# Key products shared between GpSimd and VectorE in a hybrid decoder step

## Chip, cores and metric

The kernel runs on one core of a Trainium2 chip. The metric is the device time of one execution in microseconds. Five engines matter: TensorE (PE; its weight loads are PEld), VectorE (DVE, `V` in the code), ScalarE (ACT, `S`), GpSimd (POOL, `G`) and SyncE (SP, `Q`), which issues most of the DMAs.

## What is computed

One inference step of a decoder trunk of two layers (`DEPTH` 2, `D_MODEL` 1024) for a prompt of 512 rows and for 8 samples of 8 rows, which share the weights. Cut to what matters, with the cache used by the sample rows alone:

```
h = rmsnorm(x, norm1); proj = h @ w_in
q, k, v, u, ga, gb = split(proj)             # 12 heads of 64, 3 groups of 4
o_a = dilated_mixture(rope(q), [cache; rope(k)], [cache; v])   # windows 128/1, 512/4, 2048/16
o_b = pool_branch(u)                         # causal means over 2, 4, 8, 16 rows
x = x + (sigmoid(ga) * (o_a @ w_pa) + sigmoid(gb) * (o_b @ w_pb)) @ w_o
x = x + square(relu(rmsnorm(x, norm2) @ w_up)) @ w_down
```

The scores of a sample row are dot products of its query with cached keys. Per pair of heads (`p` = 0 or 1) the kernel forms them without TensorE, as a product of keys and a broadcast query, summed over the 64 elements of each head.

## The kernel before

All activations are held transposed, as 8 tiles of 128 x 576 (512 prompt columns and 64 sample columns). Weights arrive as `raw` tiles; ScalarE rounds a tile to `wh`, VectorE subtracts to get the rest `wl`, and TensorE multiplies three times per weight (`wnext`, `wplain`, `gemm`, `gemm8`). So every weight tile needs one ScalarE pass and one VectorE subtraction with two SBUF inputs.

Per layer the order on TensorE is: the qkv units d, a, b, e, c of p = 0 and then d, a, b, c of p = 1 (`qkv`), four gates u for the pooling branch, eight gates gb with their projections of `ob`, eight gates ga with their projections of `oat` (these begin with `until("D", 1)`, that is, after the decode attention of p = 1), the output projection, and the MLP.

Beside this main order run side generators, resumed at each `tick` of the main order: `unit_out` (evacuates a qkv unit: `nat` on ScalarE, `dn` on VectorE), `prompt(p)` (attention of the prompt: scores `sp`, row maxima, `exps`, a small chain `xt`, `ex`, `ct`, `cc`, then `weigh`, `flip`, `pv`), `decode(p, qb)` (attention of the samples), `windows` and `lin` (pooling branch). The program order on every engine is the order of emission. A planner decides it: each engine is a `Lane` with a modelled time `t`, advanced by a fixed cost and a rate; a generator yields the modelled time at which it wants to go on (`after`, `ready`, or a number of us). `Lane` models what GpSimd does to VectorE in one line: a VectorE instruction with more than one large SBUF input is lengthened, to at most 1.4 times its streaming time, while GpSimd is modelled busy.

`decode` for one `p` does this. It loads keys in chunks `kc` (one of 8 rows per lane of window 128, and alternately windows 512 and 2048 for c = 0..3). For each c and each of the three groups it forms two products `prod` (tokens c and c + 4) on GpSimd, 128 x 1024 for two groups and 128 x 512 for the third, so 24 per `p` and 96 in all; `fold` sums each on VectorE with a `tensor_reduce` into `SC`, one to two products behind; the generator goes on every 2.2 us (1.1 us for the small ones). `prod` has three buffers. Then follow the products with the new keys (`prodn`, VectorE), the softmax of `SC`, and the weighted sum of values on TensorE, whose operands `pb` (from `SC` and constant masks) GpSimd multiplies out. The decode of p = 1 starts after the end of that of p = 0 (`("D", 0)`), since `SC` has one buffer.

GpSimd also adds up the squares for the norms (`square`: all but the last of 8 adds; at the very start it forms four of the eight squares and adds them itself), adds `mB` to `tb` in seven of eight ga steps, and in the MLP issues the 112 copies of the caches, paced by a 1 x 1 copy `pace<-beat` that waits for VectorE.

Of the kernel before, what the change touches and what calls it, by code (L numbers as in the profile page):

```python
# [91 lines left out]
def hybrid_decoder_kernel(ctx: ExitStack, tc: tile.TileContext, a, o):  # L92
# [230 lines left out]
    def size(x):  # L323
        n = 1
        for d in x.shape[1:]:
            n *= d
        return n

    class Lane:
        def __init__(self, eng, fixed, rate):  # L330
            self.eng, self.fixed, self.rate, self.t, self.table = eng, fixed, rate, 0.0, None

        def __getattr__(self, name):
            op = getattr(self.eng, name)

            def run(*args, **kw):
# [5 lines left out]
                d = max(size(x) for x in outs + ins) / self.rate  # L342
                if self is V and G.t > t and sum(x.space != PSUM and size(x) > 128 for x in ins) > 1:
                    d = min(1.4 * d, 0.7 * d + G.t - t)
                t += self.fixed + d
# [9 lines left out]
    wire = [0.0]  # L355
# [25 lines left out]
    def after(*lanes, lag=0.2):  # L381
        return "at", max([now[0]] + [x.t for x in lanes]) + lag

# [56 lines left out]
    def square(x, sqs, k):  # L440
        if k == 0:
            S.activation(sqs, x, AF.Square)
        else:
            t = tp.tile([128, NT], F32, tag="t", name="sq")
            S.activation(t, x, AF.Square)
            (V if k == 7 else G).tensor_add(sqs, sqs, t)
# [88 lines left out]
    for l in range(L):  # L535
# [18 lines left out]
        if l == 0:  # L554
# [44 lines left out]
            G.tensor_mul(sqs, xt[0], xt[0])  # L599
            for k in range(2, NK, 2):  # L600
                t = xp.tile([128, NT], F32, tag="even", name="even", bufs=2)
                G.tensor_mul(t, xt[k], xt[k])
                G.tensor_add(sqs, sqs, t)

            def begin():
                odd = xp.tile([128, NT], F32, name="odd")
                for k in range(1, NK, 2):
                    t = odd if k == 1 else xp.tile([128, NT], F32, tag="sq", name="sq", bufs=3)
                    S.activation(t, xt[k], AF.Square)
                    if k > 1:  # L610
                        V.tensor_add(odd, odd, t)
                V.tensor_add(sqs, sqs, odd)
                x_stack.close()
                dec_open()
                yield after(V, G)
# [115 lines left out]
        def prompt(p):  # L731
# [85 lines left out]
            def weigh(hh, j):  # L817
                c0 = 128 if j == 0 else 0
                pj = P[:, hh, j]
                V.tensor_scalar(out=pj[:, c0:256], in0=pj[:, c0:256], scalar1=cc[:, 5, j, hh:hh + 1], scalar2=None,  # L820
                                op0=ALU.mult)
                V.tensor_scalar(out=pj[:, 256:], in0=pj[:, 256:], scalar1=cc[:, 2, j, hh:hh + 1], scalar2=None,
                                op0=ALU.mult)
# [25 lines left out]
            yield after(V)  # L849
            for n in range(9):  # L850
# [6 lines left out]
                yield after(V, S, lag=-0.2)  # L857
# [56 lines left out]
        def decode(p, qb):  # L914
# [10 lines left out]
            yield (6.0, 0.5)[p]  # L925
            pend = []

            def fold(depth):
# [693 lines left out]
```

## Time and profile before

| | |
|---|---|
| median of 3 runs | 1784.4 us (1782.09 to 1785.99) |
| the profiled execution | 1783.08 us, span 1781.3 us from first to last instruction |
| mean granted TensorE clock | 0.958 of 2.4 GHz |
| decode of p = 0, layer 0 and 1 | products start at 90.2 and 963.2 us |
| decode of p = 1, layer 0 and 1 | products start at 240.9 and 1112.3 us |

Busy time of an engine is the time that one of its instructions is recorded as running, and includes time in which it is held up inside. PEclk is the share of full clock granted to TensorE; at 0.5 it ran at 1.2 GHz. Times in the text are from the first instruction of the profiled execution.

### The profile page before, as it was taken

Reading aid. Unit: us, or ns where it says so; the run is one execution under the profiler, and the core shown is the slowest. Engines: PE = TensorE matmul, PEld = TensorE weight load, DVE = VectorE, ACT = ScalarE, POOL = GpSimd, SP = SyncE. Lnnn points to the kernel's source line nnn. Section 1 sums busy time; section 2 is a strip of 40 time slices with the busy share of each in tenths; the row PEclk is TensorE's granted clock in tenths of the full one; section 3 lists DMA queues with packets and bytes.
Section 4 is the critical chain, followed back from the end, with each engine's and each line's share of the span. In section 5 each row is a group of like instructions: output and inputs, shape, how many; then the busy total and the mean of one; then the engine's idle time right before and its main releaser. Section 6 shows DMA issues by size and latency. Waiting matters only on the chain.

```text
span 1781.3 us, 30681 instructions
## 1 busy us (share of the span) xinstructions
PE 1650.3 (93%) x12608; PEld 1598.0 (90%) x12608; DVE 1179.5 (66%) x1801; ACT 668.1 (38%) x1142; POOL 429.0 (24%) x461
## 2 busy tenths in 40 slices
PE   8969988999879999999998889799997999999995
PEld 7968878899879999999998788798997999999995
DVE  6488679535767666676636967893456666676663
ACT  5513422223453433444444233221344433444443
POOL 2083238210211111111103802742111111111202
PEclk9979999999999999999998899899998999999998
DMA  4462743624325455542426365334251455544521
GB/s 170 159 193 84 223 122 109 180 64 131 115 98 188 166 177 189 188 163 94 130 80 218 125 199 171 99 104 145 78 187 42 156 177 189 189 163 167 171 74 54
DMA packets 140005, 255.21 MB, mean 143 GB/s; under 512 B 9660, under 2 KB 100284, under 8 KB 137034
## 3 DMA queue, kind: packets, MB, share of 16 engines
q1 hardware_dynamic: 135498, 198.46, 34.9%
q0 software_dynamic: 3648, 53.98, 8.4%
q8 instruction: 99, 1.62, 0.4%
q10 hardware_dynamic: 720, 0.82, 0.1%
q14 instruction: 40, 0.33, 0.1%
HBM read 239.40 MB, written 74.87 MB: 176 GB/s over the span
## 4 chain that ended last, share of the span: by engine, by line
PE 70%; DVE 13%; ACT 5%; issue 5%; DMA 3%; POOL 2%; SPq 1%; POOLq 0%; DVEq 0%; ACTq 0%
PE mm L375 37%; PE pa L375 10%; PE mmq L375 7%; PE pc L375 5%; DVE wl L352 4%; PE pb L375 2%; POOL prod L352 2%; PE po L375 2%; DVE SC L352 2%; ACT wh L352 2%; PE psd L375 1%; DMA kc<-in_c 1%; DVE cc L352 1%; DVE xr L352 1%; PE O L375 1%
## 5 line engine op out<-in xcount | busy, mean ns | idle before, releaser
L375 PE MATMUL mm<-m,wh 128*128 128x256 f32 (+1 forms) x2560 | 450.8, 297 | 4.7 <-DVE xr L352 3.3
L375 PEld LDWEIGHTS mm<-m,wh 128*128 128x128 f32 x2560 | 386.6, 189 | 6.1 <-issue 2.5
L352 DVE TENSOR_TENSOR wl<-raw,wh 128x1024 fp32r<-128x1024 f32 (+2 forms) x195 | 246.0, 1262 | 69.0 <-ACT wh L352 66.1
L375 PE MATMUL mm<-m,wl 128*128 128x320 f32 (+1 forms) x1280 | 281.5, 297 | 10.2 <-DVE wl L352 10.2
L352 POOL TENSOR_TENSOR prod<-kc,qb 128x1024 f32<-128x1024 f32 (+1 forms) x96 | 208.5, 2204 | 220.8 <-DMA kc<-in_c 191.1
L352 ACT CAST wh<-raw 128x1024 fp32r<-128x1024 f32 (+2 forms) x195 | 183.0, 938 | 200.9 <-PE mm L375 77.0
L352 ACT CAST wh<-rawu 128x512 fp32r<-128x512 f32 (+1 forms) x158 | 123.1, 783 | 352.8 <-DVE rawu L352 302.1
L375 PE MATMUL mm<-a,wh 128*128 128x256 f32 (+1 forms) x1280 | 238.1, 310 | 5.4 <-DVE tb L352 5.4
L375 PE MATMUL mmq<-wh,a 128*128 128x256 f32 x1152 | 225.1, 296 | 4.4 <-DVE a L352 2.3
L375 PEld LDWEIGHTS mm<-m,wl 128*128 128x128 f32 x1280 | 217.5, 189 | 11.1 <-DVE wl L352 11.1
L375 PEld LDWEIGHTS mm<-a,wh 128*128 128x128 f32 x1280 | 197.8, 197 | 12.4 <-issue 11.5
L375 PEld LDWEIGHTS mmq<-wh,a 128*128 128x128 f32 x1152 | 187.9, 200 | 7.2 <-DVE a L352 2.9
L352 POOL COPY pace<-beat 1x1 f32<-1x1 f32 x112 | 61.6, 550 | 548.0 <-DVE beat L352 548.0
L352 DVE TENSOR_TENSOR wl<-rawu,wh 128x512 fp32r<-128x512 f32 (+1 forms) x158 | 143.7, 912 | 66.9 <-ACT wh L352 64.5
L352 DVE TENSOR_TENSOR xr<-xr,mm 128x576 f32<-128x576 f32 (+2 forms) x152 | 108.7, 716 | 114.5 <-PE mm L375 108.2
L375 PE MATMUL pa<-h,wh 128*128 128x288 f32 x896 | 181.6, 295 | 0.0
L375 PE MATMUL mmq<-wl,a 128*128 128x256 f32 x576 | 167.9, 291 | 0.0
L375 PEld LDWEIGHTS pa<-h,wh 128*128 128x128 f32 x896 | 144.9, 188 | 0.0
L375 PE MATMUL mm<-a,wl 128*128 128x256 f32 (+1 forms) x640 | 140.5, 302 | 0.0
L375 PE MATMUL pa<-h,wl 128*128 128x288 f32 x448 | 132.4, 296 | 0.0
L375 PEld LDWEIGHTS mmq<-wl,a 128*128 128x128 f32 x576 | 115.2, 200 | 0.0
L352 DVE TENSOR_REDUCE SC<-prod 128x16 f32<-128x1024 f32 (+1 forms) x96 | 96.4, 1030 | 25.5 <-POOL prod L352 25.3
(214 smaller groups left out, 2622.4 us busy)
## 6 DMA issues: line engine op xcount, KB each, us to landing
out_s<-in_c POOLq DMA_DIRECT2D x64, 508.0 KB, 5.0
rawu<-in_wup SPq DMA_DIRECT2D x60, 512.0 KB
raw<-in_wd SPq DMA_DIRECT2D x60, 512.0 KB
kc<-in_c SPq DMA_DIRECT2D x40, 512.0 KB
raw<-in_wq SPq DMA_DIRECT2D x35, 512.0 KB
kc<-in_c SPq DMA_DIRECT2D x64, 256.0 KB
out_s<-in_c POOLq DMA_DIRECT2D x32, 504.0 KB, 5.4
raw<-in_wgb SPq DMA_DIRECT2D x16, 512.0 KB
```

Source lines behind the costliest of these rows:

```text
L352: return op(*args, **kw)
L375: return self.eng.matmul(out, w, x, **kw)
```

## The change

- In `decode`, each pair of products is split: VectorE forms the one of token c, GpSimd that of token c + 4. A 1 x 1 copy on GpSimd that reads the first product (`pace`) is put ahead of the second, so that GpSimd starts after VectorE has finished the first. Behind these, VectorE sums the previous pair's second product and this pair's first one. The fixed pace is replaced by `ready` (keys and queries there, plus 0.6 us) and by `lull`, which puts a step off until VectorE's modelled backlog is under 0.3 us, for at most 5 us.
- The operands `pb` of the value sums go from GpSimd to VectorE (72 instructions).
- The adds of squares go to VectorE (18 between the layers and in the output projections, and at the start ScalarE forms all eight squares and VectorE adds them). Those of the last stage (`last`) stay.
- The adds of `mB` go to VectorE (14).
- `weigh` (64 instructions that scale the attention rows of the prompt) goes from VectorE to ScalarE.
- In the planner, a VectorE instruction whose operands are all in SBUF, other than `tensor_reduce`, now waits for a GpSimd instruction that has started, and GpSimd waits for such a VectorE instruction.
- `windows` starts its transposes 3 us after it was opened or 1 us after its state has arrived, in place of 8 us.

```diff
@@ -328,7 +328,7 @@
         def __init__(self, eng, fixed, rate):
-            self.eng, self.fixed, self.rate, self.t, self.table = eng, fixed, rate, 0.0, None
+            self.eng, self.fixed, self.rate, self.t, self.table, self.last = eng, fixed, rate, 0.0, None, 0.0
@@ -339,10 +339,15 @@
                 t = max(self.t, due(outs, ins, self))
-                d = max(size(x) for x in outs + ins) / self.rate
-                if self is V and G.t > t and sum(x.space != PSUM and size(x) > 128 for x in ins) > 1:
-                    d = min(1.4 * d, 0.7 * d + G.t - t)
-                t += self.fixed + d
+                d = self.fixed + max(size(x) for x in outs + ins) / self.rate
+                if self is V and name != "tensor_reduce" and all(x.space != PSUM for x in ins):
+                    if G.t - G.last <= t:
+                        t = max(t, G.t)
+                    port[0] = t + d
+                elif self is G:
+                    t = max(t, port[0])
+                self.last = d
+                t += d
                 f = args[2] if name == "activation" else None
@@ -352,7 +357,7 @@
-    wire = [0.0]
+    wire, port = [0.0], [0.0]
@@ -380,6 +385,12 @@
         return "at", max([now[0]] + [x.t for x in lanes]) + lag
+
+    def lull(limit=5.0):
+
+        end = now[0] + limit
+        while V.t > now[0] + 0.3 and now[0] < end:
+            yield "at", min(max(V.t - 0.2, now[0] + 0.1), end)
@@ -443,7 +454,7 @@
             S.activation(t, x, AF.Square)
-            (V if k == 7 else G).tensor_add(sqs, sqs, t)
+            V.tensor_add(sqs, sqs, t)
@@ -596,23 +607,15 @@
-            G.tensor_mul(sqs, xt[0], xt[0])
-            for k in range(2, NK, 2):
-                t = xp.tile([128, NT], F32, tag="even", name="even", bufs=2)
-                G.tensor_mul(t, xt[k], xt[k])
-                G.tensor_add(sqs, sqs, t)
-
             def begin():
-                odd = xp.tile([128, NT], F32, name="odd")
-                for k in range(1, NK, 2):
-                    t = odd if k == 1 else xp.tile([128, NT], F32, tag="sq", name="sq", bufs=3)
+                for k in range(NK):
+                    t = sqs if k == 0 else xp.tile([128, NT], F32, tag="sq", name="sq", bufs=3)
                     S.activation(t, xt[k], AF.Square)
-                    if k > 1:
-                        V.tensor_add(odd, odd, t)
-                V.tensor_add(sqs, sqs, odd)
+                    if k:
+                        V.tensor_add(sqs, sqs, t)
                 x_stack.close()
                 dec_open()
-                yield after(V, G)
+                yield after(V)
                 yield from stats(sqs, True, ("a", 0))
@@ -817,10 +820,8 @@
                 pj = P[:, hh, j]
-                V.tensor_scalar(out=pj[:, c0:256], in0=pj[:, c0:256], scalar1=cc[:, 5, j, hh:hh + 1], scalar2=None,
-                                op0=ALU.mult)
-                V.tensor_scalar(out=pj[:, 256:], in0=pj[:, 256:], scalar1=cc[:, 2, j, hh:hh + 1], scalar2=None,
-                                op0=ALU.mult)
+                S.activation(pj[:, c0:256], pj[:, c0:256], AF.Copy, scale=cc[:, 5, j, hh:hh + 1])
+                S.activation(pj[:, 256:], pj[:, 256:], AF.Copy, scale=cc[:, 2, j, hh:hh + 1])
@@ -846,7 +847,7 @@
             weigh(*steps[0])
-            yield after(V)
+            yield after(S)
             for n in range(9):
@@ -854,7 +855,7 @@
                     flip(*steps[n])
-                yield after(V, S, lag=-0.2)
+                yield after(S, lag=0.1)
             split(oat[:, :, 0:NP], O)
@@ -922,30 +923,34 @@
             got += [chunk(p, *todo.pop(0), 0) for _ in range(2)]
-            yield (6.0, 0.5)[p]
-            pend = []
-
-            def fold(depth):
-                while pend and (len(pend) > depth or pend[0][4] <= now[0]):
-                    pr, s0, n, t, _ = pend.pop(0)
-                    V.tensor_reduce(out=SC[:, s0:s0 + n, t], in_=pr.rearrange("p s (h d) -> p s h d", h=2),
-                                    axis=AX.X, op=ALU.add)
+            late = []
+
+            def product(eng, kk, g, n, t):
+                pr = dp.tile([128, n, 128], F32, tag="prod", name="prod", bufs=3)
+                eng.tensor_mul(pr, kk, qb[:, t, g].unsqueeze(1).to_broadcast([128, n, 128]))
+                return pr
+
+            def fold(pr, s0, n, t):
+                V.tensor_reduce(out=SC[:, s0:s0 + n, t], in_=pr.rearrange("p s (h d) -> p s h d", h=2),
+                                axis=AX.X, op=ALU.add)
...
                     kk = got.pop(0) if g else k1
-                    for i in range(2):
-                        t = c + 4 * i
-                        pr = dp.tile([128, n, 128], F32, tag="prod", name="prod", bufs=3)
-                        G.tensor_mul(pr, kk[:, 4 * i:4 * i + 4] if g == 2 else kk,
-                                     qb[:, t, g].unsqueeze(1).to_broadcast([128, n, 128]))
-                        pend.append((pr, s0, n, t, G.t + 0.3))
-                        fold(2)
-                        yield "pace", (2.2 if n == 8 else 1.1)
+                    yield ready(kk, qb, lag=0.6)
+                    yield from lull()
+                    ks = [kk[:, 4 * i:4 * i + 4] if g == 2 else kk for i in range(2)]
+                    one = product(V, ks[0], g, n, c)
+                    G.tensor_copy(pace[:, 1:2], one[0:1, 0, 0:1])
+                    two = product(G, ks[1], g, n, c + 4)
+                    while late:
+                        fold(*late.pop(0))
+                    fold(one, s0, n, c)
+                    late.append((two, s0, n, c + 4))
                     if g and todo:
...
             yield after(G)
-            fold(0)
+            fold(*late.pop(0))
             yield ("kvn", p)
@@ -993,8 +998,8 @@
                 pb = dp.tile([128, 8, 8, 16], F32, tag="prod", name="pb", bufs=3)
-                G.tensor_mul(pb[:, 0:n], *spread(s0, n, None))
-                yield after(G)
+                V.tensor_mul(pb[:, 0:n], *spread(s0, n, None))
+                yield after(V)
                 for s in range(n):
@@ -1010,8 +1015,8 @@
                     t = c + 4 * i
-                    G.tensor_mul(pb[:, :, i], *spread(8, 8, t))
-                    G.tensor_mul(qs[:, 4 * i:4 * i + 4], SC[:, 16:20, t].unsqueeze(2).to_broadcast([128, 4, 16, 2]),
+                    V.tensor_mul(pb[:, :, i], *spread(8, 8, t))
+                    V.tensor_mul(qs[:, 4 * i:4 * i + 4], SC[:, 16:20, t].unsqueeze(2).to_broadcast([128, 4, 16, 2]),
                                  C("bdz")[:, 8 - 8 * i:24 - 8 * i].unsqueeze(1).unsqueeze(3)
@@ -1019,7 +1024,7 @@
             at = dp.tile([128, 4, 128], F32, tag="at", name="at", bufs=1)
-            yield after(G)
+            yield after(V)
             for c in range(4):
@@ -1080,7 +1085,8 @@
         def windows(sn):
-            yield 8.0
+            yield 3.0
+            yield ready(sn, lag=1.0)
             ptr = trp.tile([128, 512], F32, tag="tr", name="trs")
@@ -1209,7 +1215,7 @@
             V.scalar_tensor_tensor(out=t, in0=t, scalar=1.0, in1=ps, op0=ALU.add, op1=ALU.mult)
-            (V if f == 7 else G).tensor_add(t, t, mB[f])
+            V.tensor_add(t, t, mB[f])
             m = mp_.tile([128, 2, NT], F32R, tag="m", name="m")
```

## Rows read from the trace of the kernel before

**Rows 1.** The page, part 1: busy time of two engines, share of the span, instructions.
```profile
PE 1650.3 (93%) x12608; PEld 1598.0 (90%) x12608; DVE 1179.5 (66%) x1801; ACT 668.1 (38%) x1142; POOL 429.0 (24%) x461
```
**Rows 2.** Busy time by stretch: the four stretches in which GpSimd multiplies cache keys.
```profile
core 0: us, PE busy (x) PEld busy (x) DVE busy (x) ACT busy (x) POOL busy (x), PEclk, DMA share, GB/s
...
90.00:138.00 48.00, 33.19 (x218) 32.14 (x217) 43.33 (x41) 8.38 (x15) 39.99 (x19) 0.75 0.58 176
...
240.00:316.00 76.00, 60.45 (x420) 57.99 (x417) 67.44 (x72) 19.21 (x33) 51.59 (x24) 0.91 0.33 94
962.00:1010.00 48.00, 35.65 (x240) 34.68 (x239) 42.32 (x41) 8.39 (x15) 41.27 (x19) 0.79 0.60 183
...
1112.00:1186.00 74.00, 60.37 (x399) 58.02 (x398) 66.63 (x69) 17.50 (x31) 50.55 (x24) 0.86 0.33 96
```
**Rows 3.** Waits of TensorE, 86 to 330 us: us in total, times, longest us.
```profile
PE psd L375 <- DVE dn L352: 9.3, 1, 9.3
PE mm L375 <- DVE tb L352: 6.3, 3, 3.8
PE ex L375 <- DVE xt L352: 5.5, 1, 5.5
```
**Rows 4.** Timeline of VectorE, 86 to 132 us: start, us, what.
```profile
96.22 3.74 DVE L352 TENSOR_TENSOR xt<-stt,const 128x32 f32<-128x32 f32 x2
...
100.48 1.21 DVE L352 TENSOR_TENSOR wl<-raw,wh 128x1024 fp32r<-128x1024 f32 x1
...
114.45 7.49 DVE L352 TENSOR_TENSOR wl<-raw,wh 128x1024 fp32r<-128x1024 f32 x1
...
129.47 0.47 DVE L352 SCALAR_TENSOR_TENSOR dn<-psd,rs,dt 64x256 f32<-64x256 f32 x1
```
**Rows 5.** Timeline of GpSimd, 86 to 132 us.
```profile
112.29 8.56 POOL L352 TENSOR_TENSOR prod<-kc,qb 128x512 f32<-128x512 f32 x4 [1.31 <-DVE SC L352]
```
**Rows 6.** Timeline of VectorE, 190 to 240 us, while GpSimd multiplies no keys.
```profile
207.02 0.50 DVE L352 TENSOR_TENSOR xt<-stt,const 128x32 f32<-128x32 f32 x2
...
223.23 0.83 DVE L352 SCALAR_TENSOR_TENSOR pg<-s,u 128x512 f32<-128x512 f32 x2
```
**Rows 7.** Group of VectorE, 90 to 138 us: count | busy us, mean ns.
```profile
L352 DVE TENSOR_TENSOR wl<-raw,wh 128x1024 fp32r<-128x1024 f32 x4 | 11.8, 2944 | 0.0
```
**Rows 8.** Groups of VectorE, 240 to 316 us.
```profile
L352 DVE TENSOR_TENSOR wl<-raw,wh 128x512 fp32r<-128x512 f32 (+1 forms) x9 | 16.4, 1822 | 0.0
L352 DVE SCALAR_TENSOR_TENSOR pg<-s,u 128x512 f32<-128x512 f32 (+1 forms) x4 | 6.1, 1561 | 0.1
```
**Rows 9.** Groups of GpSimd over the whole span, by form.
```profile
L352 POOL TENSOR_TENSOR prod<-kc,qb 128x1024 f32<-128x1024 f32 x64 | 165.0, 2602 | 189.7 <-DMA kc<-in_c 171.5 <-DVE SC L352 12.8 <-DVE cc L352 5.3
...
L352 POOL TENSOR_TENSOR prod<-kc,qb 128x512 f32<-128x512 f32 x32 | 44.6, 1409 | 31.1 <-DMA kc<-in_c 19.6 <-DVE SC L352 11.4
...
L352 POOL TENSOR_TENSOR sqs<-sqs,sq 128x576 f32<-128x576 f32 x18 | 25.7, 1429 | 164.5 <-ACT sq L352 164.5
```
**Rows 10.** Groups of VectorE over the whole span, by form.
```profile
L352 DVE TENSOR_REDUCE SC<-prod 128x16 f32<-128x1024 f32 x64 | 76.1, 1209 | 25.5 <-POOL prod L352 25.3
...
L352 DVE TENSOR_SCALAR P<-P,cc 128x256 f32<-128x256 f32 x56 | 22.4, 442 | 0.0
...
L352 DVE TENSOR_TENSOR prodn<-kvn,qb 128x768 f32<-128x768 f32 x16 | 15.2, 948 | 0.0
...
L352 DVE TENSOR_TENSOR tb<-tb,mB 128x576 f32<-128x576 f32 x2 | 1.5, 758 | 0.1
```
**Rows 11.** Group of ScalarE over the whole span, by form.
```profile
L352 ACT ACTIVATE nat<-mmq,rs 128x256 f32<-128x256 f32 x64 | 25.1, 476 | 45.1 <-PE mmq L375 44.1 <-DVE rs L352 1.1
```
**Rows 12.** The tile pace: ns of one, min/median/max, first and last start.
```profile
L352 POOL COPY pace<-beat x112: 174/512/1714, 517.3 to 1689.9; 1x1 f32<-1x1 f32 x112
```
**Rows 13.** Timeline of ScalarE, 363 to 365 us.
```profile
364.20 0.21 ACT L352 CAST oat<-po 64x64 fp32r<-64x64 f32 x1 [0.28 <-DVE oat L352]
```
**Rows 14.** Timeline of TensorE, 371 to 373 us.
```profile
372.40 0.70 PE L375 MATMUL mm<-oat,wh 128*128 128x256 f32 x4
```

## The prediction, made before the change was run

> **What bounds the kernel now.** I read the busy times first. TensorE is busy 93% of the span, VectorE 66%, GpSimd 24% [rows 1]. The kernel is bound by TensorE, so a change can gain only where TensorE idles or runs at the lower clock. I then asked for busy time in the four stretches in which GpSimd multiplies cache keys [rows 2]. I call them S1 (90 to 138), S2 (240 to 316), S3 (962 to 1010) and S4 (1112 to 1186); S1 and S3 belong to the decode of p = 0, S2 and S4 to that of p = 1. TensorE's idle time there is length minus PE busy: 14.8, 15.6, 12.4 and 13.6, together 56.3 us. The granted clock is 0.75, 0.91, 0.79 and 0.86, so TensorE was at the lower level for 2 x (1 - clock) x length: 24.0, 13.7, 20.2 and 20.7 us, always after it had idled. Of each such stretch half is lost where TensorE had work. If all idle time fell inside them, the loss would be half of the rest: 4.6, 0, 3.9 and 3.5 us; if none did, 12.0, 6.8, 10.1 and 10.4. No row says how much, so I take the middle: 8.3, 3.4, 7.0 and 7.0 us. In all there are some 82 us to be had (68 to 96).
>
> The waits name the cause: TensorE waits 9.3 us for `dn`, 5.5 us for `xt`, 6.3 us for `tb`, all on VectorE [rows 3]. VectorE's timeline says why it was late. Two `xt` products of 32 elements took 3.74 us, and a subtraction `wl` 7.49 us, where the same one took 1.21 us shortly before; `dn` stood behind that one and took only 0.47 us itself [rows 4]. While `wl` stood still, GpSimd ran four products back to back, 112.29 to 120.85 [rows 5]. With GpSimd away from keys the same two `xt` took 0.50 us [rows 6]. So VectorE is not slow, it is held, and held through a whole run of GpSimd's products.
>
> The Trainium skill (SBUF — State Buffer, Who interferes with whom) has such a VectorE instruction and GpSimd exclude each other until the first one finishes, and `tensor_reduce` never held. By that, `wl` would lose one product of some 2.6 us at most and take 3.8 us, and 3.7 us of the wait for `dn` would have another cause and stay; the trace shows 7.49 us, and the measurement decides.
>
> **The change, part by part.** The profiled execution took 1783.1 us, 1.3 under the median of 1784.4, and the sum is made against it.
>
> *Products.* GpSimd keeps 48 of 96: 2.60 us each, 1.41 us the small ones [rows 9]. VectorE gets 48. It has no such row; the nearest are its product with the new keys, 0.95 us for 768 elements [rows 10], and `wl`, 1.21 us for 1024 [rows 4]. On that line the small ones are 0.69 us. Per decode that adds 8 x 1.21 + 4 x 0.69 = 12.4 us. The two sums that follow, 2 x 1.21 us [rows 10], lie beside GpSimd's product, which starts when VectorE's ends; a `tensor_reduce` has the same time everywhere. GpSimd can then hold VectorE only with the last part of one product, about 0.17 to 0.5 us of copy [rows 12] plus 2.60 less 2.42, and never with four in a row.
>
> *S1 and S3.* To be had: 14.8 + 8.3 + 12.4 + 7.0 = 42.5 us. Left over: a pair occupies VectorE for 1.21 + 2.42 = 3.63 us, behind which `xt` and `dn` can still be queued, on average 1.8 us, four such waits in the two layers: 7.3 us. Gain 35 us (ends: 42.5 - 14.5 - 15.3 = 13, if every wait is the full 3.63 and the clock costs what it costs now; 42).
>
> *S2 and S4.* VectorE is busy 67.4 of the 76 us of S2 [rows 2]. Held in this: nine `wl` at 16.4 us, which unheld are 0.69 to 1.21 each, some 8.5, so 7.9; four `pg` at 6.1 [rows 8], which unheld are 2 x 0.83 [rows 6], so 4.4. 67.4 - 12.3 + 12.4 = 67.5 us: as full as before. If VectorE is full, S2 can shrink by 76 - 67.5 = 8.5 us, and by 8.0 more because decode of p = 1 ends at 364.4 while TensorE first needs it at 372.4 [rows 13, 14]. Ends 0 and 16.5 per layer (19 is to be had); I take 10, 20 for two layers.
>
> *GpSimd's wait on VectorE* is new: the 1 x 1 copy. Behind it on GpSimd stand only the product and, in other stages, nothing; who waits is the next pair's sum. It costs no time on TensorE but lengthens the decode by up to 12 x 0.5 us; the cover is the 8.0 us above.
>
> *The rest, each taken at nothing.* 18 adds of squares: 1.43 us on GpSimd [rows 9], 0.76 on VectorE [rows 10]; VectorE's path changes by between 18 x 0.76 = +13.7 (nothing was held) and 18 x (0.76 - 1.43) = -12 (all were); cover is VectorE's idle third. 14 adds of `mB`: +10.6 us on VectorE, with ScalarE waiting 0.7 us less each; same cover. The start: between 0 and -4 us. `pb`: 72 small products on VectorE, some 20 us by its rate, in stretches after the keys, where GpSimd no longer holds it. `weigh`: VectorE loses 22.4 us (56 at 0.44, [rows 10]), ScalarE gains 56 at about 0.48 [rows 11]; ScalarE is busy 8.4 of 48 us in S1 [rows 2]; behind it queue `wh` roundings and `PT` copies, and if that cover went, 1 us per step of 8 would show. `windows` earlier: 0 to -5 us, not counted. No DMA is added; key loads stay on SP's queue behind the pair that frees their buffer.
>
> Sum: 35 + 20 = 55 us. 1783.1 - 55 + 1.3 = 1729.4, forecast **1730 us**. Its own range: gain from 13 (S1, S3 low, S2, S4 nothing) to 42 + 33 + 9 for the side terms, so 1700 to 1771.
>
> **The rivals.** *Load, not lock.* VectorE carries as much as before: in S2 67.5 for 67.4. In S1, `wl` loses 11.8 - 4 x 1.21 = 7.0 us [rows 7] and `xt` 3.2, while 19 of 24 products' share [rows 2], 9.8 us, comes on: 42.9 for 43.3. If TensorE's waits go with VectorE's load, nothing is gained but some us of clock, and the time is 1782. For it: VectorE is nearly full in all four. Against: TensorE's longest waits are for instructions of 0.25 and 0.47 us behind held ones [rows 4], and the new order puts products only where VectorE's modelled backlog is short.
>
> The Trainium skill (Perfetto Trace Analysis, Optimizing Scalar/DVE Operations) says that moving work between GpSimd and VectorE might not help, as they share a port; by that the time would stay at 1784. Against it stands that a product takes 2.60 us there and some 1.21 here, so the shared time falls.
>
> *Decode late, slower.* Each of 12 steps per decode may be put off 5 us, plus 0.6. A pair's chain is 1.21 + 0.34 + 2.60, the small one 0.69 + 0.34 + 1.41: 8 x 4.15 + 4 x 2.44 = 43 us. With every wait at its limit the decode takes 43 + 12 x 5.6 = 110 us against the 76 of S2, where all 24 products ran [rows 2], plus 8.0 to spare. TensorE then stops at `until("D", 1)` for 26 us in each layer; S2 and S4 gain nothing, S1 and S3 keep 35: 1784.4 + 52 - 35 = 1801. It decides from a mean wait of 4.9 us a step: 43 + 12 x 4.9 = 84 + 17.5. For it: VectorE has only 8.5 us free in S2, so the backlog is seldom short. Against: the waits go with VectorE's other work, 67.5 less 12.4 of products and some 25 of sums, so 30 us in S2, which is some 2.5 us a step.
>
> **How the numbers follow.** Forecast 0.74 (1700 to 1771). Load 0.11, around 1782: 0.04 of it faster, 0.05 the same, 0.02 slower. Decode late 0.13, around 1801. More than I can find, under 1700: 0.02. A measurement here tells 0.2% (3.6 us) from no change. Faster 0.74 + 0.04 + 0.02 = 0.80, the same 0.05, slower 0.13 + 0.02 = 0.15. The range takes in the forecast and the load case: 1700 to 1784, with some 0.15 above and 0.02 below.
>
> **What would show it.** Right: longest `wl` near 1.2 + 0.5 us in S1 and none over 4; the waits for `dn` and `xt` under 2 us; PEclk in S1 and S3 above 0.9; VectorE's busy time in S2 about the same. For the late decode: a wait of TensorE for `oat` of 10 us or more ahead of the first `mm<-oat`. For load: waits for `dn` and `xt` as long as now with no VectorE instruction stretched. Wrong altogether: GpSimd's products starting ahead of VectorE's, or `wl` still held.

## The result, and the profile after

The changed kernel took 1764.6 us (median of 4, 1757.9 to 1768.7) against 1783.9 of the kernel before beside it: ratio 0.989, 95% interval 0.986 to 0.992. The sign was right and the time lies in the range, but the gain is 19 us where 55 were forecast. The profiled execution took 1757.9 us, so the stages below compare it with the 1783.1 us of before; their difference is 25.2, some 6 more than that of the medians.

The page of the changed kernel, busy times, beside [rows 1]:

```profile
## 1 busy us (share of the span) xinstructions
PE 1632.0 (93%) x12608; PEld 1585.7 (90%) x12608; DVE 1158.4 (66%) x1892; ACT 695.4 (40%) x1210; POOL 229.7 (13%) x350
```

GpSimd lost 199 us; VectorE, with 48 products, the sums and `pb` on top and the weighting (22.4 us, [rows 10]) gone, is busy 21 us less. An instruction that is held counts as busy. Taking each VectorE instruction's time above the fastest tenth of its form and adding up, I get 120 us held before and 26 after.

Busy time in the four stretches of key products, beside [rows 2]; the first and third belong to p = 0:

```profile
88.00:143.00 55.00, 50.54 (x430) 48.08 (x430) 46.57 (x54) 26.40 (x50) 26.29 (x24) 0.97 0.52 161
244.00:314.00 70.00, 54.27 (x361) 51.86 (x361) 58.62 (x68) 16.86 (x26) 26.82 (x25) 0.88 0.30 90
950.00:1005.00 55.00, 50.06 (x424) 47.76 (x425) 46.02 (x54) 26.03 (x49) 26.02 (x24) 0.97 0.52 160
1104.00:1174.00 70.00, 54.39 (x363) 51.98 (x362) 58.26 (x69) 17.09 (x27) 26.44 (x25) 0.88 0.29 91
```

In the first and third the granted clock rose from 0.75 and 0.79 to 0.97, and TensorE idles 4.5 and 4.9 us. In the second and fourth it idles 15.7 and 15.6 us at 0.88: no better than before.

What TensorE waits for in the whole span, beside [rows 3]:

```profile
PE mm L380 <- DVE ud L357: 17.0, 2, 9.1
PE lq L380 <- ACT pn L357: 13.4, 2, 6.7
PE po L380 <- DMA kc<-in_c: 10.5, 11, 2.4
PE mm L380 <- DVE tb L357: 9.6, 4, 2.8
```

`dn` (2.5 us left, ahead of the first products) and `xt` are gone from the head of the list; `ud`, `pn` and `kc` have taken their places. GpSimd's and VectorE's timelines at the products, beside [rows 4, 5]:

```profile
97.26 0.17 POOL L357 COPY pace<-prod 1x1 f32<-1x1 f32 x1 [1.41 <-DVE prod L357]
97.40 2.42 POOL L357 TENSOR_TENSOR prod<-kc,qb 128x1024 f32<-128x1024 f32 x1
102.17 0.17 POOL L357 COPY pace<-prod 1x1 f32<-1x1 f32 x1 [2.35 <-DVE prod L357]
102.31 2.43 POOL L357 TENSOR_TENSOR prod<-kc,qb 128x1024 f32<-128x1024 f32 x1
...
98.78 2.13 DVE L357 TENSOR_TENSOR wl<-raw,wh 128x1024 fp32r<-128x1024 f32 x1
100.83 1.21 DVE L357 TENSOR_TENSOR prod<-kc,qb 128x1024 f32<-128x1024 f32 x1
101.96 2.33 DVE L357 TENSOR_REDUCE SC<-prod 128x16 f32<-128x1024 f32 x2
```

GpSimd starts after VectorE's product, one product at a time; the `wl` that meets one takes 2.13 us (2.14 is the longest in that stretch), where it was 7.49. VectorE's product takes 1.21 us, as estimated.

**Where the gain went.** The layers cut at two instructions, the first matmul with `ob` and the first with `oat` (us of the profiled executions; "lost" is TensorE's idle time plus half of its busy time at the lower clock):

| stage | length before, layer 0 / 1 | after | lost before, both | after |
|---|---|---|---|---|
| A: to the first `mm<-ob` | 277.4 / 262.4 | 262.2 / 252.0 | 92.3 | 66.3 |
| B: to the first `mm<-oat` | 94.9 / 96.5 | 98.2 / 99.0 | 22.6 | 37.0 |
| C: the rest | 513.3 / 536.8 | 510.2 / 534.6 | 67.6 | 64.2 |

A gained 25.6 us, B gave back 5.8, C gained 5.3. (S1 and S3 lie in A; S2 and S4 begin in A and end in B.) Inside A, the end of the first `O` moved from 188.3 to 129.3, but then TensorE meets this (its timeline, VectorE's and SP's queue, layer 0):

```profile
187.87 1.30 PE L380 MATMUL mm<-a,wh 128*128 128x256 f32 x4 [9.10 <-DVE ud L357]
186.90 0.69 DVE L357 TENSOR_TENSOR u<-mm,rb 128x512 f32<-128x512 f32 x1 [11.73 <-DMA DV<-nat]
161.36 10.47 SPq L340 DMA_DIRECT2D kc<-in_c  x4
174.70 2.54 SPq L340 DMA_DIRECT2D raw<-in_wgb  x1
177.29 2.60 SPq L340 DMA_DIRECT2D DV<-nat  x1
```

The pooling branch's `u` is written where `nat` lay, and the store of `nat` to `DV` stood behind key and weight loads on SP's queue. Before, that store was issued at 193.9 and `u` followed at 203.0; TensorE, still in the attention of the prompt, did not notice. So the first `O` came 59 us forward, `u` only 16. The waits are 17.0 us in two layers, and the matmuls behind run at the lower clock (1.30 us for four). The chain that ends the second decode shows B's loss (changed kernel, 320 to 366; start, length, what):

```profile
333.48 7.39 PE mm L380 x54
...
341.90 1.71 DVE pb L357 x2
343.61 0.04 issue
343.65 2.65 PE po L380 x32
346.30 0.05 issue
346.35 3.92 DMA kc<-in_c
350.27 0.04 issue
350.31 0.70 PE po L380 x8
351.01 0.02 issue
351.03 1.20 SPq L340
352.23 0.05 issue
352.28 5.30 DMA kc<-in_c
```

and its two ends, on ScalarE and TensorE, beside [rows 13, 14]:

```profile
361.13 0.21 ACT L357 CAST oat<-po 64x64 fp32r<-64x64 f32 x1 [0.28 <-DVE oat L357]
360.42 1.31 PE L380 MATMUL mm<-oat,wh 128*128 128x256 f32 x4
```

Before, the decode ended at 364.7 and the first matmul with `oat` came at 372.3, after the last one with `ob` (356.7) and the gates behind it. Now `ob` ends at 327.6, the gates behind it at 340.9 and the decode at 361.6: from 340.9 on TensorE has only the decode's own matmuls, and between them it waits, mostly for value loads (4.7 us for `kc` there).

### The profile page after: what moved, and what is told of

It reads as the page before. It is cut to its first block, busy times and chain, and to the rows that moved or that the text cites. A ratio compares the mean times of both kernels' runs of the same rounds, so it can differ in the third digit from the quotient of the medians.

```text
span 1756.2 us, 30640 instructions
## 1 busy us (share of the span) xinstructions
PE 1632.0 (93%) x12608; PEld 1585.7 (90%) x12608; DVE 1158.4 (66%) x1892; ACT 695.4 (40%) x1210; POOL 229.7 (13%) x350
## 4 chain that ended last, share of the span: by engine, by line
PE 78%; DVE 9%; DMA 6%; ACT 4%; issue 2%; SPq 1%; POOL 1%; POOLq 0%; DVEq 0%; ACTq 0%
PE mm L380 42%; PE mmq L380 10%; PE pa L380 10%; PE pc L380 5%; PE pb L380 2%; DVE wl L357 2%; DMA DV<-nat 2%; PE po L380 2%; PE psd L380 2%; DMA kc<-in_c 1%; ACT wh L357 1%; SPq L340 1%; PE sp L380 1%; PE O L380 1%; DVE SC L357 1%
## 5 line engine op out<-in xcount | busy, mean ns | idle before, releaser
L357 DVE TENSOR_TENSOR wl<-raw,wh 128x1024 fp32r<-128x1024 f32 (+2 forms) x195 | 218.5, 1122 | 83.4 <-ACT wh L357 80.1
L380 PE MATMUL mm<-a,wh 128*128 128x256 f32 (+1 forms) x1280 | 233.9, 306 | 22.4 <-DVE ud L357 17.0
L380 PE MATMUL mmq<-wh,a 128*128 128x256 f32 x1152 | 215.8, 288 | 1.6 <-ACT a L357 0.7
L380 PEld LDWEIGHTS mmq<-wh,a 128*128 128x128 f32 x1152 | 179.7, 192 | 4.3 <-issue 1.4
L380 PE MATMUL mmq<-wl,a 128*128 128x256 f32 x576 | 163.4, 284 | 0.0
L380 PEld LDWEIGHTS mm<-a,wl 128*128 128x128 f32 x640 | 110.8, 194 | 0.0
L380 PEld LDWEIGHTS mmq<-wl,a 128*128 128x128 f32 x576 | 110.4, 192 | 0.0
L380 PE MATMUL pc<-h,wh 128*128 128x288 f32 x512 | 104.5, 295 | 0.0
```

The costliest lines, as they stand in the source:

```text
L357: return op(*args, **kw)
L380: return self.eng.matmul(out, w, x, **kw)
```

## The experiments

Each kernel was compared with the kernel before on its chip. "Changed" means the kernel after. The table is from the profiled executions, layer 0, in us; the ratio is of the timed runs with its 95% interval.

| run | median | ratio | first `mm<-ob` | last `mm<-ob` | decode p = 1 ends | first `mm<-oat` |
|---|---|---|---|---|---|---|
| before | 1783.9 | 1 | 277.4 | 356.7 | 364.7 | 372.3 |
| changed | 1764.6 | 0.989 [0.986, 0.992] | 262.2 | 327.6 | 361.6 | 360.4 |
| e1 all GpSimd | 1759.5 | 0.985 [0.983, 0.987] | 254.9 | 321.1 | 361.7 | 360.5 |
| e2 all VectorE | 1756.5 | 0.983 [0.981, 0.986] | 248.0 | 311.7 | 359.0 | 357.7 |
| e3 store elsewhere | 1761.9 | 0.986 [0.984, 0.989] | 261.2 | 326.5 | 360.9 | 359.7 |
| e4 half the keys | 1730.9 | 0.970 [0.967, 0.973] | 264.4 | 338.8 | 338.1 | 351.3 |
| f1 model alone | 1808.6 | 1.016 [1.012, 1.019] | 282.4 | 354.3 | 382.6 | 381.4 |
| f2 no wait | 1791.2 | 1.006 [1.003, 1.009] | 281.0 | 366.2 | 364.9 | 378.7 |
| f3 short wait | 1793.0 | 1.007 [1.004, 1.009] | 294.8 | 367.9 | 352.1 | 380.4 |
| f4 split, no moves | 1762.6 | 0.991 [0.988, 0.994] | 245.5 | 313.3 | 356.2 | 355.0 |
| g1 wait alone | 1791.1 | 1.005 [1.003, 1.007] | 287.7 | 361.5 | 380.4 | 381.6 |
| g2 third gate set | 1756.5 | 0.986 [0.983, 0.988] | 261.6 | 327.5 | 363.8 | 362.6 |
| g3 same, all VectorE | 1756.4 | 0.986 [0.983, 0.988] | 253.2 | 318.1 | 368.1 | 366.9 |
| g4 same, kernel before | 1788.2 | 1.004 [1.003, 1.006] | 279.2 | 358.9 | 366.9 | 380.9 |
| h1 model and wait | 1809.0 | 1.014 [1.011, 1.016] | 271.7 | 337.6 | 384.7 | 383.5 |
| h2 early decode | 1747.5 | 0.980 [0.978, 0.982] | 264.6 | 329.9 | 357.2 | 356.0 |
| h3 early, third set | 1747.8 | 0.980 [0.978, 0.982] | 263.8 | 331.0 | 360.2 | 362.2 |
| h4 same, all GpSimd | 1734.0 | 0.973 [0.970, 0.976] | 261.5 | 322.2 | 355.8 | 354.7 |
| i1 h1 and weighting | 1777.7 | 0.996 [0.994, 0.998] | 263.7 | 321.7 | 369.2 | 368.0 |
| i2 e1, weighting back | 1777.6 | 0.994 [0.992, 0.997] | 264.6 | 331.6 | 371.4 | 370.2 |

The first `mm<-oat` starts 1.2 us before the decode's recorded end (behind its last matmul), or when the gate sets behind the last `mm<-ob` are through (12.5 us after it in e4, f2 and f3; longer where the decode's matmuls lie between them), whichever is later. The next four ask who made the gain and who took it back.

**e1.** The split undone, all else as changed.

```diff
-                    one = product(V, ks[0], g, n, c)
-                    G.tensor_copy(pace[:, 1:2], one[0:1, 0, 0:1])
+                    one = product(G, ks[0], g, n, c)
```

> The changed kernel with all 96 key products back on GpSimd, everything else as changed. Theory (the lock was what cost, and the changed kernel took it away): VectorE is held again, TensorE's waits for dn and xt in the qkv units of p = 1 come back (over 4 us each, against none now), and the time goes back to 1775 to 1790 us. Rival (VectorE's load was what cost): VectorE loses some 49 us of products, so the time falls to 1760 us or less.

A miss in time: 1759.5 us, no slower than the changed kernel. That is the rival's price, but e2 speaks against the rival's cause. Of the two waits, `dn` did not come back and `xt` did: 8.7 us in two layers, where the kernel before had 10.3 and the changed kernel none. So beside the other parts the split takes away the wait for `xt`, but brings no time. VectorE is held 75 us here, counted as above, against 26. The waits of TensorE and the timelines (GpSimd, then VectorE) show what is held:

```profile
PE ex L380 <- DVE xt L357: 8.7, 2, 4.7
...
PE psd L380 <- DVE dn L357: 2.5, 1, 2.5
...
84.55 6.03 POOL L357 TENSOR_TENSOR prod<-kc,qb 128x1024 f32<-128x1024 f32 x3 [83.61 <-PE ex L380]
95.41 11.86 POOL L357 TENSOR_TENSOR prod<-kc,qb 128x512 f32<-128x512 f32 x5 [4.83 <-DVE SC L357]
...
87.05 3.56 DVE L357 TENSOR_TENSOR cc<-cc,ct 128x8 f32<-128x8 f32 x1
...
97.52 2.65 DVE L357 TENSOR_TENSOR wl<-raw,wh 128x1024 fp32r<-128x1024 f32 x1
100.10 1.80 DVE L357 TENSOR_REDUCE SC<-prod 128x8 f32<-128x512 f32 x2
105.46 2.90 DVE L357 TENSOR_TENSOR wl<-raw,wh 128x1024 fp32r<-128x1024 f32 x1 [3.56 <-ACT wh L357]
```

GpSimd still runs three and five products in a row. During the five, VectorE has `tensor_reduce`, nothing to do, or a held `wl` that no wait of TensorE follows; `dn` is not among them. During the three, the small chain ahead of `xt` is held.

**e2.** All products on VectorE, so nothing of the keys holds it.

```diff
-                    two = product(G, ks[1], g, n, c + 4)
+                    two = product(V, ks[1], g, n, c + 4)
```

> The changed kernel with all 96 key products on VectorE, none on GpSimd. Theory (lock): no wait of TensorE for dn or xt over 4 us in the qkv units; the decode of p = 1 gets longer by some us, and the time is 1760 to 1775 us. Rival (load): 49 us more on VectorE make it slower, 1775 us or more, with waits for VectorE's instructions in the qkv units.

1756.5 us with 13 us held: less than the theory's 1760, and the rival (load) falls, as the 48 further products on VectorE did not make it slower. In `mm<-ob` it is 14 us ahead of the changed kernel, in `mm<-oat` only 2.7.

**e3.** The store that `u` waits for, for p = 1, issued by GpSimd instead of SP.

```diff
-            Q.dma_start(DV.rearrange("(j p) f -> p j f", j=4), nat)
+            (G if p else Q).dma_start(DV.rearrange("(j p) f -> p j f", j=4), nat)
```

> The changed kernel with the store of the c unit's values of p = 1 (DV<-nat) issued from GpSimd's queue, which is empty there, in place of SyncE's. Theory (part of the gain is given back at a store that stands late in SyncE's queue): TensorE's wait for ud (9.1 and 7.8 us) falls under 3 us in both layers, and the time falls by 5 to 25 us, less than the wait if the end of the decode of p = 1 becomes the bound. Rival (the store is late for its own duration, not for its place in the queue): the wait stays over 6 us and the time within 4 us of the changed kernel's.

The rival: the wait for `ud` fell from 17.0 to 13.0 us only, so most of it is not the place in SP's queue; the time overlaps with that of the changed kernel.

**e4.** The second decode shortened.

```diff
-            for c in range(4):
+            for c in range(4 - 2 * p):
...
```

> The changed kernel with only half of the key products and sums in the decode of p = 1 (tokens 0, 1, 4, 5; the scores of the other cached keys are left at zero). Theory (the rest of the gain is given back where TensorE waits for the end of the decode of p = 1): TensorE's stop ahead of the first mm<-oat goes, the value sums move back beside the ga and gb gates, and the time falls by 20 to 40 us. Rival (TensorE does not lose there): the time falls by under 8 us.

As expected: by the medians 34 us less than the changed kernel. The decode ends at 338.1 and the `ob` side sets the first `oat` again. Part of that may be VectorE's 12 products and 24 sums fewer (both layers), GpSimd's 12 products and four key loads fewer, so this bounds what the end of the decode is worth from above.

**f1.** The kernel before with only the planner's new cost model (`Lane.run` of the diff above).

> The kernel before, with only the cost model of the program generator exchanged: VectorE's read-only products wait in the model for a GpSimd instruction that has started, and GpSimd waits for VectorE. No instruction on any engine is added, removed or moved to another engine; only the order in which the program is written out differs. Theory 'order' (the gain of about 20 us comes from TensorE's order being written with the right delays, so that pieces which hang on VectorE stand further back): at most 1768 us, and TensorE's waits for dn, xt and tb in 85-140 us fall from 20 us to under 8 us. Theory 'lull' (the gain comes from GpSimd's products being started only when VectorE is quiet): 1778 to 1790 us, those waits stay over 14 us.

Neither: 28 us slower than before. **f2.** The changed kernel with the product loop of before:

```diff
-                    yield ready(kk, qb, lag=0.6)
-                    yield from lull()
...
+                        yield "pace", (2.2 if n == 8 else 1.1)
```

> The changed kernel with the product loop of before (all products on GpSimd, one each 2.2 or 1.1 us by the generator's clock, no waiting for a quiet VectorE); the planner's model, the squares, sums and weighting stay as changed. Theory 'lull': 1775 us or more, TensorE's waits for dn and xt at 85-140 us over 8 us again, held weight splits (wl up to 5 us or more). Theory 'order': within 5 us of the run with all products on GpSimd (1755 to 1765 us), those waits under 6 us.

1791.2 us against the 1759.5 of e1, which differs by the wait (and the pairing that goes with it): 32 us by the medians, 38 by the ratios. The waits of TensorE are back (f2, 84 to 190):

```profile
PE psd L380 <- DVE dn L357: 12.8, 2, 11.1
PE trq L384 <- ACT PT L357: 5.8, 4, 3.6
PE ex L380 <- DVE xt L357: 3.7, 1, 3.7
```

and over the whole span

```profile
PE psd L380 <- DVE dn L357: 26.0, 5, 11.1
```

VectorE is held 71 us here and 75 in e1, and TensorE waits for `xt` alike (8.6 and 8.7 us), but for `dn` 26.0 us against 2.5: not how long VectorE is held decides, but which instruction is.

**f3.** The changed kernel with a shorter wait in the second decode.

```diff
-                    yield ready(kk, qb, lag=0.6)
-                    yield from lull()
+                    yield ready(kk, qb, lag=(0.6, 0.2)[p])
+                    yield from lull((5.0, 1.0)[p])
```

> The changed kernel with the wait for a quiet VectorE cut from at most 5.0 to at most 1.0 us in the decode of the second head pair (p=1) alone, and 0.2 instead of 0.6 us behind a landed chunk. Theory (what gave the gain back is the end of that decode, at 361.7 us, because its pairs wait for VectorE): its products end by about 300 us instead of 313, the split of its output ends at 350 us or earlier, and the time is 1735 to 1750 us. Rival (the pairs then collide with VectorE's splits of weights and TensorE waits for those instead): 1757 us or more, with waits for wl, lq or ud grown by 8 us or more.

The rival. The products end at 293 and the decode at 352, but the pooling branch stands behind them on VectorE (f3, TensorE's waits, 240 to 366):

```profile
PE lp L380 <- DVE ob L357: 22.7, 2, 21.4
PE lq L380 <- ACT pn L357: 18.1, 1, 18.1
```

So VectorE in that stretch is a trade: the decode sooner, `ob` later.

**f4.** The changed kernel with the squares after the first norm, the sums of `mB` and `pb` back on GpSimd and the weighting back on VectorE (the last two not shown).

```diff
-            V.tensor_add(sqs, sqs, t)
+            (V if k == 7 else G).tensor_add(sqs, sqs, t)
...
-            V.tensor_add(t, t, mB[f])
+            (V if f == 7 else G).tensor_add(t, t, mB[f])
```

> The changed kernel with the squares, mlp sums and spread weights back on GpSimd and the weighting of values back on VectorE; the division of the products, the waiting for a quiet VectorE and the planner's model stay. Theory (these moves are worth little by themselves): 1758 to 1770 us. Rival (the weighting and sums carry the gain): 1775 us or more, with a wait of TensorE for xt of 3 us or more in each layer's O of the first head pair.

1762.6 us: beside the split, the moves are worth nothing that can be measured.

**g1.** The kernel before with the pairs and their wait, both products on GpSimd, the old model.

> The kernel before with one thing of the change: its product loop starts each pair of products, both still on GpSimd, only when the chunk has landed and the planned end of VectorE's queue is near (at most 5.0 us of waiting). The planner's cost model, the squares, the sums and the weighting are those of before. Theory (this wait alone carries the gain): 1752 to 1766 us, TensorE's waits for dn and xt in 85-140 us under 10 us together. Rival (the wait works only with the changed cost model or with the work taken off VectorE): 1772 us or more.

The rival: 1791.1 us. **h1.** Model and wait together, no work moved between engines.

> The kernel before with two things of the change: the planner's new cost model and the pairs that wait for a quiet VectorE; both products of a pair on GpSimd, and squares, sums and weighting where they were before. So no instruction changes its engine. The model alone gave 1808.6 us, the wait alone 1791.1. Theory (model and wait carry the gain together, the engines of the work little): 1755 to 1768 us, TensorE's waits for dn and xt in 85-140 us under 10 us. Rival (the weighting on ScalarE or the work taken off GpSimd is a third condition): 1773 us or more.

The rival again, 1809.0 us: `xt` and `dn` hold TensorE less (`xt` 5.9 us in all and `dn` 4.1 in two layers, 16.9 for `dn` before), but the products of p = 1 end at 340 (308 before, 316 in e1) and the decode at 384.7. A likely reason, not tried apart, is that VectorE is too seldom quiet: its weighting takes 764 ns an instruction here, 355 in f4 (groups of VectorE, 84 to 150, h1 and f4):

```profile
L357 DVE TENSOR_SCALAR P<-P,cc 128x256 f32<-128x256 f32 (+1 forms) x16 | 11.5, 764 | 0.0
```

```profile
L357 DVE TENSOR_SCALAR P<-P,cc 128x256 f32<-128x256 f32 (+1 forms) x16 | 4.9, 355 | 0.0
```

**i1.** h1 with `weigh` on ScalarE, as in the diff above.

> The kernel before with three things of the change: cost model, wait for a quiet VectorE, and the weighting on ScalarE; all products, squares and sums on the engines of before. Model and wait alone gave 1809.0 us: with GpSimd's products, the weighting (mean 764 ns where 355 is its time beside the split) and the rest, VectorE was not quiet often enough and the products of the second decode ended at 340 us. Theory (any step that takes the held work off VectorE makes model and wait pay: weighting on ScalarE is enough): 1755 to 1772 us, end of the second decode at 355-365 us. Rival (the squares and sums off GpSimd were what mattered): 1785 us or more.

**i2.** e1 with `weigh` back on VectorE.

> The run with all products on GpSimd (1759.5 us), with the weighting back on VectorE; model, wait, and the squares and sums on VectorE stay. Theory (weighting on ScalarE or the split of the products is needed): 1785 to 1810 us, end of the second decode at 375 us or later. Rival (squares and sums off GpSimd were what mattered): 1770 us or less.

Both 1778 us, between theory and rival. So with all products on GpSimd, by the ratios times 1784, the weighting is worth 32 us (h1 to i1), the squares, sums, `pb`, the new start and the earlier `windows` together 35 (h1 to i2), all of them 52 (h1 to e1); the split without them 41 (h1 to f4, which keeps the earlier `windows` and the new start), and on top of them nothing (e1 to changed). They stand in for each other. That each does so by freeing VectorE, so that the wait finds its gaps, fits these rows; it was not tried apart.

**g2, g3, g4.** One more gate set ahead of `until("D", 1)`, in the changed kernel, with all products on VectorE, and in the kernel before.

```diff
-    LEADA = (2, 3, 4, 5, 6, 7, 8, 8)
+    LEADA = (3, 4, 5, 6, 7, 8, 8, 8)
```

> The changed kernel with one more gate product set ahead of TensorE's stop for the decoded values (three instead of two; the same matmuls in another order). Theory (TensorE stands or runs at half clock in 328-362 us because it has no work left before the stop): the stop's idle and half clock are filled, end of decode stays at 360 to 366 us, 1738 to 1750 us. Rival (the AV matmuls and their loads of kc set that stretch by themselves and slip behind the added matmuls): 1755 us or more, end of decode 370 us or later.

> All products on VectorE and one more gate product set ahead of the stop. Theory: this version has no wait for ud (17 us in the changed kernel) and its ob ends 16 us earlier, so the extra work fits wholly: 1728 to 1745 us. Rival as for the lead alone: 1750 us or more.

> The kernel before with the same extra gate product set ahead of the stop. There decode ended (364.7 us) before the first matmul on its values could start (ob ended 356.7 us and two gate sets followed), so nothing stands at the stop: theory 1778 to 1790 us, no change. Rival (the longer lead helps or hurts whatever the decode does, through the order of the weights' loads): 1770 us or less, or 1795 us or more.

g2 is 8 us faster than the changed kernel by the medians, less than expected, and the intervals overlap; the decode's end stayed (363.8), so the rival's condition did not hold either. g3 got nothing over e2: there the decode's end went from 359.0 to 368.1 with the added matmuls. g4 is as expected, 0.4% slower than before: its first `oat` moved 8.6 us back, as nothing stood at the stop.

**h2.** Of the changed kernel's second decode, the eight products with new keys and the first pair of cache products set ahead of the end of the first decode.

```diff
-            SC = dp.tile([128, 23, 8, 2], F32, tag="SC", name="SC", bufs=1)
+            SC = dp.tile([128, 23, 8, 2], F32, tag="SC", name="SC", bufs=2)
...
+                    if p == 1 and c == 0 and g == 2:
+                        yield ("D", 0)
```

> The changed kernel; in the second head pair's decode the products with the eight new keys and the first pair of cache products are set ahead of the end of the first decode (second SC buffer), into VectorE's free time at 200-244 us. The same arithmetic. Theory (the end of the second decode sets when TensorE can go on): it falls from 361.7 to 342-354 us, and the time to 1738-1752 us. Rival (behind it the AV loads and ob's end at 328 us plus two gate sets of 13 us hold TensorE to about 354 anyway, so little comes of it): decode's end falls as much, the time stays at 1755 us or more.

> As the run before, with the third gate set ahead of the stop too (which alone gave 1756.5 us). Theory: both together remove the half clock and idle at the stop: 1732 to 1748 us. Rival: 1753 us or more.

> As the run before, but all products on GpSimd (which alone gave 1759.5 us, without the wait for ud). Theory: VectorE holds less work at 244-315 us and TensorE does not wait for ud, so it is at least as fast as the run before: 1730 to 1748 us. Rival (held VectorE instructions in that stretch eat it up): over 1752 us.

h2's time fell as expected, to 1747.5; its decode ends at 357.2, not by 354. The first `pb` came 15 us sooner (326.7 against 341.9), and the value matmuls now run beside the gates, so B takes 91.4 us in layer 0 instead of 98.2. h3, within what was expected, added nothing to h2: with the third set the gates end at 362.2, behind the decode. h4, the same with all products on GpSimd, is the fastest but for e4, which leaves work out: **1734.0 us, 2.7% under the kernel before**. TensorE waits there 2.7 us for `kc` in all, and not for `ud` (14.7 us in h2); which of its 14 us under h3 come from that was not tried apart. Its page:

```profile
PE 1632.5 (94%) x12608; PEld 1584.6 (91%) x12608; DVE 1152.5 (67%) x1852; ACT 695.8 (40%) x1210; POOL 333.8 (19%) x350
```

Idle time plus half of busy time at the lower clock is 135.7 us in it, 167.3 in the changed kernel and 182.5 before.

## Why the prediction was right in sign and wrong in size

**S1 and S3, "Gain 35 us": near in size, wrong in the agent.** A lost 92.3 - 66.3 = 26.0 us less, with a new wait of 17.0 us in it. e1, e2 and f4 have no such wait: in layer 0, e1 lost 29.2 in A against 51.2 before, 22.0 less, and e2 and f4 bring the first `ob` 29.4 and 31.9 us forward, the changed kernel 15.2. So a gain of that size was there; how much of it lies in S1 and S3 alone is not shown, as A is longer than they are. Most signs came as named: in S1 and S3 no wait for `dn` or `xt`, clock 0.97, longest `wl` 2.14. Wrong was the agent. The reading that VectorE is held through a run of GpSimd's products holds; that halving the products is needed to free it does not. With all of them on GpSimd (e1) the wait for `dn` goes as well, and only that for `xt` stays (8.7 us). What carries the gain is the step put off until VectorE is quiet (f2 against e1), with work taken off VectorE (h1 against i1, i2, e1 and f4); f1, f2, f3, g1 and h1 each lack one or both of these, f3 in the second decode only, and all are slower than before. Whether the new model is needed is not shown: no run has the wait and the moves under the old one, and added to the wait alone it cost time (g1 1.005, h1 1.014).

**S2 and S4, "I take 10, 20 for two layers": the step that failed.** Measured: B took 5.8 us more, and A and B together 19.8 less, where 55 were forecast for the four stretches. I put down 8.0 us of it as slack, "because decode of p = 1 ends at 364.4 while TensorE first needs it at 372.4". But 372.4 was the end of another chain, which hangs on S1: my own gain of 17 us a layer there had to bring `ob` and the first need for the decode forward. It did, by 29 us (356.7 to 327.6), and the cover of 8 became a shortfall of 21.5 (gates through 12.5 us behind 327.6, decode's end 361.6). Meanwhile the run of products did not get shorter: 12 steps in 69.3 us (244.0 to 313.3) are 5.8 us each. I had priced a pair's chain at 3.6 us on average (43 / 12) and the mean wait at 2.5 us; the wait came out (5.8 - 3.6 = 2.2). Their sum, 12 x 6.1 = 73 us, was set against the 76 of S2, but S2 was the window and not the run: before, the products took 67.5 us, from 240.9 to 308.4. The last ones, before and after:

```profile
299.50 8.89 POOL L352 TENSOR_TENSOR prod<-kc,qb 128x512 f32<-128x512 f32 x4
...
310.87 2.45 POOL L357 TENSOR_TENSOR prod<-kc,qb 128x1024 f32<-128x1024 f32 x1
```

So the run starts 3.1 us later and is 1.8 longer, and the decode's end comes only 3.1 us sooner, as the tail behind the products, which the sum left out, shrank from 56.3 to 48.3. Nor was VectorE as full as that step supposed, and the sign of it (busy time in S2 about the same) failed: it is busy 58.6 of 70 us, where 67.5 of 76 had been set down. That the end of the decode is what took the gain back is shown from both sides: shortening or advancing it pays (e4 34 us, h2 17), and a sooner `ob` alone does not (e2 and f4, 29.4 and 31.9 us sooner, bring the first `oat` of layer 0 only 14.6 and 17.3 forward, the changed kernel 11.9).

**What was not priced: the waits next in line.** The 17.0 us for `ud` and the 13.4 for `pn` (whose buffer waits for a store of its own) are stalls that the earlier order uncovered; the prediction priced waits on VectorE alone, none for the stores on SP's queue.

**The rivals.** *Load, not lock* (1782) fell as a whole: all, half or none of the key products on VectorE (e2, changed, e1; held 13, 26 or 75 us) give 1756 to 1765. The rule of the Trainium skill (Perfetto Trace Analysis, Optimizing Scalar/DVE Operations), that moving work between GpSimd and VectorE might not help, came true for the split beside the other parts (e1 against the changed kernel), but not without them (h1 against f4, which has the new start and the earlier `windows` too). *Decode late* had the mechanism that took the gain back, but its point of decision, a mean wait of 4.9 us, was set against the old need; against the moved one 2.2 us was enough. h1 comes near that case: decode's end at 384.7, 1809 us against its 1801. f1 ends as late (382.6) with no wait for VectorE in it, so it is not that case.

**The moves, "each taken at nothing".** Beside the split that holds (f4). It is no property of the moves: without the split, the weighting is worth 32 us and the others together 35.

**Still open.** Why the model alone costs 28 us was not followed up beyond its later decode. Whether the wait for `ud` costs what it lasts was not shown: e3 shortened it by 4 us without a measurable gain, and e1, e2 and f4, which do not have it, end B at nearly the same point.

## What to carry to other kernels

A slack is the distance between two chains: if the change shortens one of them, take the slack again with the shortened chain before counting on it as cover. When several edits come together, price each with the others in place and with them away; here the split or the moves were enough beside the model and the wait, the second of them added nothing, and model and wait by themselves, each or both, made the kernel slower. And before crediting a wait to a shared resource, ask which instruction is held: 75 us held with 2.5 us of waits for `dn` (e1) gave 1759 us, 71 us held with 26.0 (f2) 1791.

## What was not expected of the hardware

A VectorE `wl` under GpSimd's products took 2.65 to 2.90 us in e1 although five products ran in a row (11.86 us), and 7.49 us before under four. In e1 a `cc<-cc,ct` of 128x8, 0.17 us in its next instance, took 3.56 us under a run of three. So how long an instruction is held is not fixed by the length of the run alone, and what makes the difference was not tried. The rule of the Trainium skill (SBUF — State Buffer, Who interferes with whom), by which the prediction had 3.8 us at most, agrees with the `wl` of e1 and of the changed kernel, but not with the 7.49 us of the kernel before, nor with e1's `cc`, which was held 3.4 us where one product takes 2.4. The 1 x 1 copy on GpSimd took 0.17 us, and the product behind it started 0.14 us after the copy's start.
